# The last channel block of the second mixer matmul, from seven-product sums to ordinary products

## The chip, the cores and the metric

The kernel runs on one core of one Trainium2 chip. The metric is the device time of one execution in microseconds (us); a run's time is that of the core. Five engines work side by side, each through its own queue in order: TensorE (PE, matmuls; PEld is its weight load), VectorE (DVE), ScalarE (ACT), GpSimd (POOL) and SyncE (SP, which here only issues DMAs). TensorE's clock is granted at one of two levels, 1.2 and 2.4 GHz; the profile gives the granted clock as a share of the higher one.

## The reference, cut to what matters

One layer of a decoder trunk is computed for 1024 prompt tokens and 32 sample tokens (8 samples of 4), with a gate per channel that is one number for the prompt and one for each sample. The change lies in the last line:

```python
x = x + gate1 * jnp.dot(mixed, w_o)
xn2 = rms_norm(x, norm2_g) * (1 + scale2) + shift2
hid = jax.nn.relu(jnp.dot(xn2, w_mlp_in))          # 1024 -> 4096 channels
x = x + gate2 * jnp.dot(hid * hid, w_mlp_out)      # 4096 -> 1024 channels
```

## The kernel before

All tensors are held transposed: channels on the 128 partitions, the T = 1056 tokens along the free axis. A float32 product is computed as three faster ones: each operand is split into a rounded high part and the rest (hi, lo), and hi·hi, hi·lo and lo·hi are summed in PSUM. ACT makes the high part (a cast), DVE or POOL subtracts it to get the low part.

Most large matmuls use a seven-product scheme on 2x2 blocks (Strassen's, in Winograd's form): seven products of sums and differences of blocks instead of eight products of the blocks. The sums of the weight blocks are made by POOL (L228 to L231) and split by ACT and DVE (L157, L161, tile wprod); `products_to` keeps this three products ahead of TensorE.

The second mixer matmul takes the 4096 hidden channels in NBLK = 8 blocks of 512. The squared hidden rows lie in DRAM (`hid_d`); `fetch` loads a block of them as quarters (tile hraw: two channel tiles of 128 by two token quarters of H = 264), and `prepare` makes the seven operands of a block out of them: `comb` (POOL, L1562) forms the differences, `high` (ACT, L1550) and `low` (DVE L1558, or POOL L1555 for the products in POOL_LOW) split them. A block is two jobs, x = 0 and 1, for output channels 0 to 511 and 512 to 1023. A job runs its seven products n = 0 to 6; a product is four PSUM groups (two output tiles j, two token halves p) of six matmuls with 264 columns (L1690 to L1692), so 24 matmuls, 168 in a job and 336 in a block. The groups go round eight PSUM banks (`tags`). The result of each group is added to a sum in SBUF, `acc[x, n]`: ACT copies it there in block 0, DVE adds it in later blocks (L1701). So each of the 14 sums runs over all eight blocks.

At the end the sums of a job have to be joined into four outputs each and added to the residual stream: the table FIN gives each step a slot and an engine. Steps j1, j6, j3, k6, j4, k2, j5 add or subtract two sums (`join`, L1624 for a whole page of 1056 columns, L1626 for halves), m1, m6, m2, m5 multiply by the gate (ACT L1605, and DVE L1608 for the 32 sample columns), a1, a6, a2, a5 add the result to the rows y1 of the output (`add`, L1612), s0 and s1 store the rows (L1638). y1[m] holds 128 output channels of the residual stream, loaded from DRAM by `load_y1` (L1588). In the last block, product 6 skips its sum: `gated` (L1593, L1597, L1601) multiplies PSUM by the gate and adds it to y1.

What sets the order: a plan that maps slots to steps. There are two slots to a product, 28 to a block; `tick(s)` writes the steps of slot s into the queues right after the matmuls of that slot, and each engine then runs its queue in order. In block b the operands of block b + 1 are prepared. Pages of 1056 columns come from a pool of NPG = 34; a page is used again once its last reader is done. `copy` issues one of 48 copies of the caches from DRAM to DRAM, 2.1 MB each in this stage, one at each of the last jobs.

`residual` (L1713, L1717, L1721) is what the attention's output projection uses to add a PSUM tile of 352 columns, times a gate, to rows of the stream: one instruction from PSUM, and for the third of the three column tiles two small ones for the samples. `gemm` (L376) runs an ordinary product as hi·hi, hi·lo, lo·hi for each channel tile, with 352 columns, its PSUM tiles here in the three banks of tag g. `prep_to` loads and splits a weight slab for it (L192 on ACT, L196 on DVE, tiles whi and wlo).

Of the kernel before, what the change touches and what calls it, by code (L numbers as in the profile page):

```python
# [17 lines left out]
P = 128  # L18
# [18 lines left out]
NBLK = 8  # L37
NG = 4
# [3 lines left out]
    (("j1", 3, "p"), ("m1", 8, ""), ("a1", 9, "p"), ("j6", 5, "p"), ("j3", 7, "d"), ("k6", 8, "pd"), ("m6", 12, ""), ("a6", 13, "d"),  # L42
     ("j4", 14, "p"), ("k2", 15, "p"), ("j5", 18, "p"), ("m2", 19, ""), ("a2", 21, "dp"), ("m5", 21, ""), ("a5", 22, "d"),
     ("s0", 14, ""), ("s1", 22, "")),
    (("j1", 3, "dp"), ("m1", 6, ""), ("a1", 11, "p"), ("j6", 5, "p"), ("j3", 7, "d"), ("k6", 10, "p"), ("m6", 10, ""), ("a6", 12, "dp"),
     ("j4", 10, "pd"), ("k2", 10, "d"), ("j5", 14, "dp"), ("m2", 11, ""), ("a2", 12, "p"), ("m5", 14, ""), ("a5", 15, "d"),
     ("s0", 14, ""), ("s1", 15, "")),
# [3 lines left out]
class Trunk:  # L51
# [374 lines left out]
    # ---- constants, adaLN modulation, first norm  # L426
# [215 lines left out]
    # ---- input projection  # L642
# [230 lines left out]
    # ---- attention over the prompt  # L873
# [168 lines left out]
    # ---- attention of the samples  # L1042
# [218 lines left out]
    # ---- whole program  # L1261

    def run(self):
# [39 lines left out]
        srcs += [(t["w_mlp_out"][2 * i], t["w_mlp_out"][2 * i + 1]) for i in range(2 * NBLK)]  # L1303
# [6 lines left out]
        # projection: gates and convolution  # L1310
# [17 lines left out]
        # projection: queries, keys, values  # L1328
# [37 lines left out]
        # convolution and attention outputs, gated  # L1366
# [62 lines left out]
        # output projection, residual, second norm  # L1429
# [73 lines left out]
        # channel mixer  # L1503
# [27 lines left out]
        raw, ops, acc, plan = {}, {}, {}, {}  # L1531

# [7 lines left out]
        def fetch(b, q):  # L1540
            if b < NBLK:
# [10 lines left out]
        def low(b, n, q):  # L1552
            h, l = ops[b, n]
            if n in POOL_LOW and (b < NBLK - 1 or n < 5):
# [27 lines left out]
        for b in range(1, NBLK):  # L1582
            prepare(b, 28 * b - 16, 4)
        y1 = {}
# [4 lines left out]

        def gated(m, c, n, src):  # L1590
            y = y1[m][:, c:c + n]
            k = min(n, NP - c)
            nc.vector.scalar_tensor_tensor(out=y[:, :k], in0=src[:, :k], scalar=gate2[:, m, 0:1], in1=y[:, :k],  # L1593
                                           op0=ALU.mult, op1=ALU.add)
            if k < n:
                tmp = self.sm.tile([P, NB, NT], F32, name="rs", tag="rs", bufs=2)
                nc.vector.tensor_tensor(  # L1597
                    out=tmp, in0=src[:, k:n].rearrange("p (b t) -> p b t", t=NT),
                    in1=gate2[:, m, 1:9].unsqueeze(2).to_broadcast([P, NB, NT]), op=ALU.mult)
                ys = y[:, k:n].rearrange("p (b t) -> p b t", t=NT)  # L1600
                nc.vector.tensor_tensor(out=ys, in0=ys, in1=tmp, op=ALU.add)  # L1601
# [33 lines left out]
        def store(x, i):  # L1635
            for j in range(2):
                m = 4 * x + 2 * i + j
                nc.sync.dma_start(out=t["yT"][:, m, :], in_=y1[m])  # L1638

        for x in range(2):  # L1640
# [7 lines left out]
                "a5": lambda x, e: adds(x, e, 5, 1, 0), "s0": lambda x, e: store(x, 0), "s1": lambda x, e: store(x, 1),  # L1648
            }
            for k, s, e in FIN[x]:  # L1650
                at(28 * NBLK - 28 + 14 * x + s, lambda x=x, e=e, f=steps[k]: f(x, e))
# [7 lines left out]
        self.last_prod = 7 * (self.npair + 4 * NBLK - NG // 2)  # L1659
# [46 lines left out]
        for s in sorted(plan):  # L1706
            tick(s)
# [213 lines left out]
```

## Time and profile before

| | |
|---|---|
| time, median of 3 runs | 2211.82 us |
| the 3 runs | 2204.81, 2211.82, 2216.55 us |
| the profiled execution: span from first to last instruction | 2215.5 us (its own time isn't given apart) |
| PE busy | 2064.9 us, 93% |
| DVE busy | 1445.6 us, 65% |
| ACT busy | 1002.2 us, 45% |
| POOL busy | 810.3 us, 37% |
| mean granted TensorE clock | 0.970 |
| second mixer matmul, first to last matmul | 1832.3 to 2200.4 us |
| from there to the end | 15.1 us |

The page shows shares over the whole span; the second mixer matmul is the last 383 us, and there the shares are others: it is read by windows of that stretch. A busy PE is not the same as a PE at full pace, since the ends of matmuls are modelled; its pace is read from the starts of matmuls that follow each other. An instruction of DVE can start while the one before it drains, so a row of equal instructions takes less than the sum of their durations; an instruction that is slowed by another engine shows as a longer instruction, not as idle time.

### The profile page before, as it was taken

To read this page: it belongs to the slowest core of one execution; us is meant where nothing else is said; L and a number is where in the kernel's file an instruction comes from. 1 tells how busy PE (TensorE), PEld (TensorE's weight loads), DVE (VectorE), ACT (ScalarE), POOL (GpSimd) and SP (SyncE) were. 2 spreads that over 40 slices of the span, in tenths; PEclk is the share of its full clock that TensorE was granted. 3 is DMA by queue.
4 is the path that set the end of the run, shared out by engine and by line. 5 is a ranking of instruction groups with operands and counts; after the bars stand their busy time and mean duration, and the time that the engine had idled before them with its cause. 6 is when DMAs were issued, how large, how long until landed. Compare 5 with 4: busy or idle time off the path is not lost.

```text
span 2215.5 us, 39124 instructions
## 1 busy us (share of the span) xinstructions
PE 2064.9 (93%) x15140; PEld 1915.1 (86%) x15140; DVE 1445.6 (65%) x3012; ACT 1002.2 (45%) x2204; POOL 810.3 (37%) x566
## 2 busy tenths in 40 slices
PE   5799999999999989999998799998999999999995
PEld 2799999889888878788787689988999999999995
DVE  4846666345556556666776568378444447999998
ACT  4532323335555645555455223255555557333332
POOL 3636565321111111100112114235333326887876
PEclk8999999999999999999999899999999999999997
DMA  7232221663144667765558985432356546564543
GB/s 278 81 121 77 60 78 60 230 232 112 48 54 54 44 145 135 148 122 106 159 137 138 207 253 175 158 122 106 107 211 240 220 167 229 198 230 172 188 164 118
DMA packets 182291, 325.87 MB, mean 147 GB/s; under 512 B 77144, under 2 KB 122456, under 8 KB 181080
## 3 DMA queue, kind: packets, MB, share of 16 engines
q1 hardware_dynamic: 181672, 323.17, 51.2%
q8 instruction: 119, 1.95, 0.5%
q14 instruction: 68, 0.56, 0.1%
q10 hardware_dynamic: 432, 0.20, 0.0%
HBM read 270.48 MB, written 112.07 MB: 173 GB/s over the span
## 4 chain that ended last, share of the span: by engine, by line
PE 48%; DVE 18%; DMA 9%; ACT 4%; issue 3%; SPq 1%; POOL 1%; another core or an unknown queue 0%; ACTq 0%; DVEq 0%; POOLq 0%
PE ps_g L376 20%; DVE acc L1701 4%; DVE wprod L161 3%; PE ps_g L263 3%; DMA st_d<-st 3%; PE ps_g L265 3%; PE ps_s L264 3%; PE ps_s L263 3%; PE ps_s L265 3%; PE ps_g L264 3%; DVE hl L1558 2%; PE ps_s L975 1%; PE ps_o L1012 1%; DVE wlo L196 1%; DMA rel<-in_rel 1%
## 5 line engine op out<-in xcount | busy, mean ns | idle before, releaser
L161 DVE TENSOR_TENSOR wprod<-wraw,wprod 128x512 fp32r<-128x512 f32 x288 | 281.4, 979 | 177.3 <-ACT wprod L157 177.1
L376 PE MATMUL ps_g<-xh,whi 128*128 128x352 f32 x1056 | 367.9, 348 | 12.4 <-ACT whi L192 4.9
L376 PE MATMUL ps_g<-xh,wlo 128*128 128x352 f32 x1056 | 346.8, 328 | 6.0 <-DVE wlo L196 5.9
L376 PE MATMUL ps_g<-xl,whi 128*128 128x352 f32 x1056 | 347.4, 329 | 2.7 <-POOL xl L405 1.8
L376 PEld LDWEIGHTS ps_g<-xh,whi 128*128 128x128 f32 x1056 | 203.3, 193 | 48.9 <-issue 25.3
L157 ACT CAST wprod<-wraw 128x512 fp32r<-128x512 f32 x288 | 170.3, 618 | 165.4 <-DVE wprod L161 113.2
L376 PEld LDWEIGHTS ps_g<-xh,wlo 128*128 128x128 f32 x1056 | 203.0, 192 | 7.5 <-DVE wlo L196 7.5
L376 PEld LDWEIGHTS ps_g<-xl,whi 128*128 128x128 f32 x1056 | 203.4, 193 | 6.1 <-POOL xl L405 3.7
L161 POOL TENSOR_TENSOR lo<-qn,hi 128x1024 fp32r<-128x1024 f32 x12 | 32.9, 2743 | 364.7 <-ACT hi L157 341.6
L196 DVE TENSOR_TENSOR wlo<-wraw,whi 128x512 fp32r<-128x512 f32 x176 | 127.9, 768 | 45.6 <-PE ps_g L376 25.4
L276 POOL TENSOR_TENSOR ps_z<-ps_z,ps_s 128x264 f32<-128x264 f32 x64 | 60.4, 946 | 251.8 <-DVE ps_s L275 251.8
L263 PE MATMUL ps_s<-th,wprod 128*128 128x264 f32 x512 | 145.7, 285 | 1.8 <-DVE ps_s L275 1.8
L263 PE MATMUL ps_g<-th,wprod 128*128 128x264 f32 x512 | 146.8, 287 | 0.0
L264 PE MATMUL ps_s<-tl,wprod 128*128 128x264 f32 x512 | 145.9, 285 | 0.0
L265 PE MATMUL ps_g<-th,wprod 128*128 128x264 f32 x512 | 145.8, 285 | 0.0
L264 PE MATMUL ps_g<-tl,wprod 128*128 128x264 f32 x512 | 145.5, 284 | 0.0
L265 PE MATMUL ps_s<-th,wprod 128*128 128x264 f32 x512 | 145.4, 284 | 0.0
L983 ACT ACTIVATE S<-S,ng 128x128 f32<-128x128 f32 (+1 forms) x192 | 84.9, 443 | 98.8 <-DVE ng L980 95.9
L192 ACT CAST whi<-wraw 128x512 fp32r<-128x512 f32 x176 | 100.0, 619 | 51.2 <-DMA wraw<-in_w_conv_out 36.7
L263 PE MATMUL ps_g<-xh,wprod 128*128 128x264 f32 x384 | 110.6, 288 | 4.1 <-ACT wprod L157 4.1
L263 PE MATMUL ps_s<-xh,wprod 128*128 128x264 f32 x384 | 110.8, 289 | 3.4 <-DVE ps_s L279 3.4
L265 PE MATMUL ps_g<-xh,wprod 128*128 128x264 f32 x384 | 110.1, 287 | 3.5 <-DVE wprod L161 3.5
(385 smaller groups left out, 6718.1 us busy)
## 6 DMA issues: line engine op xcount, KB each, us to landing
wraw<-in_w_in SPq DMA_DIRECT2D x76, 512.0 KB
wada<-in_w_ada SPq DMA_DIRECT2D x48, 512.0 KB
hid_d<-hid SPq DMA_DIRECT2D x32, 528.0 KB
hraw<-hid_d SPq DMA_DIRECT2D x64, 264.0 KB
wraw<-in_w_mlp_in SPq DMA_DIRECT2D x32, 512.0 KB
wraw<-in_w_mlp_out SPq DMA_DIRECT2D x32, 512.0 KB
kv<-in_v SPq DMA_DIRECT2D x28, 512.0 KB
wraw<-in_w_conv_out SPq DMA_DIRECT2D x24, 512.0 KB
```

The lines of the kernel that those rows point to most:

```text
L157: nc.scalar.copy(hi, src)
L161: eng.tensor_tensor(out=lo, in0=src, in1=hi.bitcast(F32), op=ALU.subtract)
L192: self.nc.scalar.copy(hi[:, s], w[:, s])
L196: self.nc.vector.tensor_tensor(out=lo[:, s], in0=w[:, s], in1=hi[:, s].bitcast(F32), op=ALU.subtract)
L263: nc.tensor.matmul(ps, hi, xh, start=(k == 0), stop=False)
L264: nc.tensor.matmul(ps, hi, xl, start=False, stop=False)
L265: nc.tensor.matmul(ps, lo, xh, start=False, stop=(k == 3))
L276: nc.gpsimd.tensor_tensor(out=z[p], in0=z[p], in1=s[p], op=ALU.add)
L376: self.nc.tensor.matmul(ps, a, x, start=(i == 0), stop=(i == n - 1))
L983: nc.scalar.activation(s, s, AF.Exp, bias=ng[:, hh:hh + 1], accum_out=sm[:, hh:hh + 1])
L1558: nc.vector.tensor_tensor(out=l[:, s], in0=raw[b, q][:, s], in1=h[:, s].bitcast(F32), op=ALU.subtract)
L1701: nc.vector.tensor_tensor(out=a, in0=a, in1=ps, op=ALU.add)
```

## The change

The last of the eight blocks leaves the seven-product scheme. Its products are now ordinary ones, 24 tiles of 12 matmuls with 352 columns (288 in place of 336 with 264), in the order of output rows m = 4, 5, 6, 7, 0, 1, 2, 3, three column tiles each. `residual` adds each tile, times the gate, straight from PSUM to y1[m]. The hidden rows of that block are loaded as they are (`fetch_last`) and split once (`split_last`, two low parts on DVE, two on POOL); there are no differences to form. Its weights are four single slabs, split by `prep_to`, in place of 14 product weights.

The sums of the seven products now run over seven blocks (NSB = 7), and the steps that join them are spread from slot -12 to slot 15 around the start of the ordinary products: those of x = 0 from 12 slots ahead of it, those of x = 1 from tile 7 on. Joins work on whole pages now, each on one engine. `gated` is gone: all sums are whole. Rows are stored after the tile that ends them, the last row in three pieces. The copies of the caches keep their number; since there are two jobs fewer, jobs 0 and 1 issue two each.

The diff, without lines that are only comments, and with two rows of the table:

```diff
+NSB = NBLK - 1
 FIN = (
-    (("j1", 3, "p"), ("m1", 8, ""), ("a1", 9, "p"), ("j6", 5, "p"), ("j3", 7, "d"), ("k6", 8, "pd"), ("m6", 12, ""), ("a6", 13, "d"),
...
+    (("j1", -12, "p"), ("j6", -10, "p"), ("m1", -9, ""), ("a1", -6, "p"), ("j3", -1, "d"), ("k6", 0, "p"), ("j4", 1, "d"), ("k2", 2, "p"),
...
-        srcs += [(t["w_mlp_out"][2 * i], t["w_mlp_out"][2 * i + 1]) for i in range(2 * NBLK)]
+        srcs += [(t["w_mlp_out"][2 * i], t["w_mlp_out"][2 * i + 1]) for i in range(2 * NSB)]
+        srcs += [(t["w_mlp_out"][4 * NSB + i],) for i in (2, 3, 0, 1)]
...
+        END = 28 * NSB
...
-            if n in POOL_LOW and (b < NBLK - 1 or n < 5):
+            if n in POOL_LOW:
...
+        def fetch_last(q):
+            raw[NSB, q] = self.page("hraw")
+            nc.sync.dma_start(out=raw[NSB, q], in_=self.hid_d[4 * NSB + q])
+
+        def split_last(q):
+            v = raw.pop((NSB, q))
+            h, l = last[q] = self.page("hh", dt=F32R), self.page("hl", dt=F32R)
+            if q % 2:
+                self.split(h, l, v, T, lo_on="pool")
+            else:
+                nc.scalar.copy(h, v)
+                for s in (slice(0, 2 * H), slice(2 * H, T)):
+                    nc.vector.tensor_tensor(out=l[:, s], in0=v[:, s], in1=h[:, s].bitcast(F32), op=ALU.subtract)
+
+        for q in range(4):
+            at(END - 26 + 2 * q, lambda q=q: fetch_last(q))
+            at(END - 9 + 2 * q, lambda q=q: split_last(q))
...
-        def gated(m, c, n, src):
...
             for k, s, e in FIN[x]:
-                at(28 * NBLK - 28 + 14 * x + s, lambda x=x, e=e, f=steps[k]: f(x, e))
+                at(END + s, lambda x=x, e=e, f=steps[k]: f(x, e))
...
-            at(28 * (NBLK - 1) + 6 + 2 * m, lambda m=m: load_y1(m))
+            at(END - 11 + 2 * m, lambda m=m: load_y1(m))
+            if m > 3:
+                at(END + 13 + m, lambda m=m: store(m))
...
-        for i in range(2 * NBLK):
+        for i in range(2 * NSB):
...
-            copy(1)
+            copy(2 if i < 2 else 1)
...
+                if n == 5:
+                    self.prep_to(ji + 1)
...
-                        elif b == NBLK - 1 and n == 6:
-                            m, c = 4 * x + j, (2 * p + 1) * H
-                            gated(m, c, H, ps)
...
-        for s in sorted(plan):
-            tick(s)
+        for n, (m, ch) in enumerate([(m, ch) for m in (4, 5, 6, 7, 0, 1, 2, 3) for ch in range(NCH)]):
+            j, s = m % 2, slice(ch * CH, (ch + 1) * CH)
+            ps = self.bank("g")
+            self.gemm(ps[:, :CH], self.wt[ji], [4 * (q // 2) + 2 * j + q % 2 for q in range(4)],
+                      [tuple(v[:, s] for v in last[q]) for q in range(4)])
+            self.residual(y1[m], ps, gate2, m, ch)
+            del ps
+            if j == 0 and ch == 1:
+                self.prep_to(ji + 1)
+            tick(END + n)
+            if m == 3:
+                store(m, s)
+            elif m < 3 and ch == 2:
+                store(m)
+            if j and ch == 2:
+                self.wt.pop(ji)
+                ji += 1
+            self.slot()
```

Where instructions stand. DVE before, in the last block: a low part of a product weight (L161), then the four sums of one product (L1701, their inputs the PSUM banks), and now and then a split of a hidden operand (L1558) or a join (L1624).

```order
L1558 TENSOR_TENSOR hl<-hraw,hh 128x528 x2
L161 TENSOR_TENSOR wprod<-wraw,wprod 128x512
L1701 TENSOR_TENSOR acc<-acc,ps_s 128x264
L1701 TENSOR_TENSOR acc<-acc,ps_pt 128x264
L1701 TENSOR_TENSOR acc<-acc,ps_g 128x264
L1701 TENSOR_TENSOR acc<-acc,ps_o 128x264
L1624 TENSOR_TENSOR acc<-acc 128x1056
```

DVE after, from the last sums to the sixth tile: L1736, L1740 and L1744 are `residual`, L195 the low part of a weight slab, L1631 a join, L1615 the gate of the samples.

```order
L1707 TENSOR_TENSOR acc<-acc,ps_o 128x264
L1631 TENSOR_TENSOR acc<-acc 128x1056
L1736 SCALAR_TENSOR_TENSOR y_24024<-ps_g,modT,y_24024 128x352 x2
L195 TENSOR_TENSOR wlo<-wraw,whi 128x512 x2
L1631 TENSOR_TENSOR acc<-acc 128x1056
L1736 SCALAR_TENSOR_TENSOR y_24024<-ps_g,modT,y_24024 128x320
L1740 TENSOR_TENSOR rs<-ps_g,modT 128x32
L1744 TENSOR_TENSOR y_24024<-y_24024,rs 128x32
L1615 TENSOR_TENSOR acc<-acc,modT 128x32 x2
L1736 SCALAR_TENSOR_TENSOR y_24059<-ps_g,modT,y_24059 128x352
L1631 TENSOR_TENSOR acc<-acc 128x1056
L1736 SCALAR_TENSOR_TENSOR y_24059<-ps_g,modT,y_24059 128x352
```

So between the readers of PSUM there now stand joins of 1056 columns, in place of the lows of product weights of 512.

POOL before, in the last block: differences of hidden quarters and their lows, the sums of weight blocks, then the joins.

```order
L1562 TENSOR_TENSOR hraw<-hraw 128x1056
L1555 TENSOR_TENSOR hl<-hraw,hh 128x1056
L1624 TENSOR_TENSOR acc<-acc 128x1056 x2
L1626 TENSOR_TENSOR acc<-acc 128x528
L1612 TENSOR_TENSOR y_24193<-y_24193,acc 128x2x264
L1612 TENSOR_TENSOR y_24238<-y_24238,acc 128x2x264
L228 TENSOR_TENSOR ws_24300<-wraw 128x512
```

POOL after, from the first joins on; the two L160 are the lows of `split_last`.

```order
L1631 TENSOR_TENSOR acc<-acc 128x1056 x2
L160 TENSOR_TENSOR hl<-hraw,hh 128x1056
L1619 TENSOR_TENSOR y_23846<-y_23846,acc 128x2x264
L1619 TENSOR_TENSOR y_23891<-y_23891,acc 128x2x264
L160 TENSOR_TENSOR hl<-hraw,hh 128x1056
L1631 TENSOR_TENSOR acc<-acc 128x1056 x2
L1619 TENSOR_TENSOR y_23846<-y_23846,acc 128x2x264
L1619 TENSOR_TENSOR y_23891<-y_23891,acc 128x2x264
L1619 TENSOR_TENSOR y_23932<-y_23932,acc 128x2x264
L1619 TENSOR_TENSOR y_23976<-y_23976,acc 128x2x264
L1631 TENSOR_TENSOR acc<-acc 128x1056 x2
```

The last pair of joins (of x = 1) and six more adds behind it run beside tiles 7 to 15; the weight blocks' sums are gone from here.

SP at the start of the second mixer matmul, before, and then the same stretch after (out_sk is a copy of a cache):

```order
L1727 DMA out_sk<-in_k3T 32x16384
L1516 DMA hid_d<-hid 128x1056 x2
L179 DMA wraw<-in_w_mlp_out 128x1024 x2
L1544 DMA hraw<-hid_d 128x2x264 x8
L1727 DMA out_sk<-in_k3T 32x16384
L179 DMA wraw<-in_w_mlp_out 128x1024 x2
```

```order
L1750 DMA out_sk<-in_k3T 32x16384 x2
L1516 DMA hid_d<-hid 128x1056 x2
L178 DMA wraw<-in_w_mlp_out 128x1024 x2
L1545 DMA hraw<-hid_d 128x2x264 x8
L1750 DMA out_sk<-in_k3T 32x16384 x2
L178 DMA wraw<-in_w_mlp_out 128x1024 x2
```

Two copies stand where one stood, ahead of the loads of the next weights and of block 1's hidden quarters.

## Rows read from the trace of the kernel before

**Rows 1.** Windows: us, length, busy us (instructions) per engine, PEclk, DMA share, GB/s
```profile
2052.00:2095.00 43.00, 41.43 (x339) 41.18 (x338) 43.00 (x77) 15.03 (x21) 34.73 (x17) 1.00 0.56 199
2136.10:2200.40 64.30, 49.17 (x338) 46.54 (x336) 63.65 (x94) 17.88 (x27) 50.65 (x27) 0.89 0.31 110
2200.40:2215.50 15.10, 0.00 (x0) 0.00 (x0) 9.44 (x17) 2.67 (x4) 5.18 (x4) 0.50 0.36 144
```

**Rows 2.** Timeline of PE: start us, duration us; first and last matmul, last block
```profile
2136.14 0.28 PE L1690 MATMUL ps_g<-hh,wprod 128*128 128x264 f32 x1
...
2199.94 0.42 PE L1692 MATMUL ps_o<-hh,wprod 128*128 128x264 f32 x1
```

**Rows 3.** What PE waited for, 2136 to 2201 us: total us, times, longest
```profile
PE ps_s L1690 <- DVE acc L1701: 6.2, 4, 3.2
PE ps_g L1691 <- DVE hl L1558: 2.8, 2, 1.7
PE ps_g L1690 <- DVE acc L1701: 2.8, 1, 2.8
```

**Rows 4.** Timeline of PE: a wait in the last block, and matmuls after it
```profile
2155.96 0.56 PE L1690 MATMUL ps_s<-hh,wprod 128*128 128x264 f32 x1 [3.15 <-DVE acc L1701]
2156.32 0.42 PE L1691 MATMUL ps_s<-hl,wprod 128*128 128x264 f32 x1
...
2158.74 0.41 PE L1690 MATMUL ps_g<-hh,wprod 128*128 128x264 f32 x1
```

**Rows 5.** The chain that ended last: one product's four sums on DVE
```profile
2140.28 1.36 DVE acc L1701 x4
```

**Rows 6.** Timeline of PE: matmuls of 352 columns, 24 starts apart
```profile
1353.76 0.32 PE L376 MATMUL ps_g<-oh,wlo 128*128 128x352 f32 x1
...
1357.62 0.32 PE L376 MATMUL ps_g<-oh,wlo 128*128 128x352 f32 x1
```

**Rows 7.** Windows: the attention's output products (L376, 12 matmuls to a tile)
```profile
1340.00:1360.00 20.00, 20.00 (x126) 20.00 (x125) 15.99 (x30) 6.34 (x14) 9.77 (x10) 1.00 0.45 142
```

**Rows 8.** Source lines: instructions, duration ns min/median/max, first and last start us
```profile
L1713 DVE SCALAR_TENSOR_TENSOR x<-ps_g,modT,x x24: 533/578/585, 1387.8 to 1484.0; 128x352 f32<-128x352 f32 x16, 128x320 f32<-128x320 f32 x8
L1721 DVE TENSOR_TENSOR x<-x,rs x8: 191/192/261, 1451.5 to 1484.7; 128x32 f32<-128x32 f32 x8
L1624 POOL TENSOR_TENSOR acc<-acc x7: 2414/2480/2923, 2148.5 to 2191.9; 128x1056 f32<-128x1056 f32 x7
L1624 DVE TENSOR_TENSOR acc<-acc x3: 1245/1258/2166, 2156.9 to 2200.3; 128x1056 f32<-128x1056 f32 x3
L1612 POOL TENSOR_TENSOR y<-y,acc x8: 1292/1593/1769, 2159.9 to 2204.6; 128x528 f32<-128x528 f32 x8
L1612 DVE TENSOR_TENSOR y<-y,acc x8: 692/708/2269, 2175.5 to 2210.1; 128x528 f32<-128x528 f32 x8
L196 DVE TENSOR_TENSOR wlo<-wraw,whi x176: 674/685/2893, 42.0 to 1525.7; 128x512 fp32r<-128x512 f32 x176
```

**Rows 9.** Timeline of the last block: two adds on DVE, and POOL beside them
```profile
2191.90 2.76 POOL L1624 TENSOR_TENSOR acc<-acc 128x1056 f32<-128x1056 f32 x1 [2.10 <-DVE acc L1624]
...
2192.96 4.00 DVE L1612 TENSOR_TENSOR y<-y,acc 128x528 f32<-128x528 f32 x2
...
2194.74 1.65 POOL L1626 TENSOR_TENSOR acc<-acc 128x528 f32<-128x528 f32 x1
```

**Rows 10.** Timeline: the last work of the kernel, on DVE and SP
```profile
2209.48 1.33 DVE L1612 TENSOR_TENSOR y<-y,acc 128x528 f32<-128x528 f32 x2 [0.80 <-ACT acc L1605]
2210.26 1.04 SPq L1638 DMA_DIRECT2D out_yT<-y  x2
```

**Rows 11.** Windows: start of the second mixer matmul, block 0
```profile
1830.00:1840.00 10.00, 6.71 (x49) 6.22 (x48) 7.56 (x9) 4.40 (x11) 7.63 (x5) 0.91 0.11 46
...
1850.00:1860.00 10.00, 10.00 (x85) 10.00 (x84) 7.08 (x6) 7.85 (x21) 8.36 (x6) 1.00 0.98 368
```

**Rows 12.** Timeline of SP in block 0: copies of the caches
```profile
1823.02 0.58 SPq L1727 DMA_DIRECT2D out_sk<-in_k3T  x1
...
1848.86 0.59 SPq L1727 DMA_DIRECT2D out_sk<-in_k3T  x1
```

More of the change, by code (lines that the diff above doesn't have):

```diff
@@ L41 @@
 FIN = (
-    (("j1", 3, "p"), ("m1", 8, ""), ("a1", 9, "p"), ("j6", 5, "p"), ("j3", 7, "d"), ("k6", 8, "pd"), ("m6", 12, ""), ("a6", 13, "d"),
[L43 to L47, printed above, removed]
[4 rows of a table added]
 )
@@ L1540, in fetch @@
         def fetch(b, q):
-            if b < NBLK:
+            if b < NSB:
                 v = raw[b, q] = self.page("hraw")
@@ L1564, in prepare @@
         def prepare(b, s0, d):
-            if b == NBLK:
+            if b == NSB:
                 return
@@ L1581, in run @@
         prepare(0, -8, 2)
-        for b in range(1, NBLK):
+        for b in range(1, NSB):
             prepare(b, 28 * b - 16, 4)
+        last = {}
+        def fetch_last(q):
[13 more added lines that the diff above has]
+            at(END - 9 + 2 * q, lambda q=q: split_last(q))
         y1 = {}
@@ L1588, in load_y1 @@
             nc.sync.dma_start(out=y1[m], in_=self.x1_d[m])
-        def gated(m, c, n, src):
[L1591 to L1601, printed above, removed]
         def scale(m, a, t):
@@ L1633, in adds, with store @@
             both(eng, lambda e, j: add(4 * x + 2 * i + j, part(x, n, j), t, e))
[L1635 to L1638, printed above, removed]
+        def store(m, s=slice(0, T)):
+            nc.sync.dma_start(out=t["yT"][:, m, s], in_=y1[m][:, s])
         for x in range(2):
@@ L1647, in run @@
                 "j5": lambda x, e: join(x, e, 5, 0, 5, ALU.subtract), "m5": lambda x, e: scales(x, 5, 1, 0),
-                "a5": lambda x, e: adds(x, e, 5, 1, 0), "s0": lambda x, e: store(x, 0), "s1": lambda x, e: store(x, 1),
+                "a5": lambda x, e: adds(x, e, 5, 1, 0),
             }
             for k, s, e in FIN[x]:
-                at(28 * NBLK - 28 + 14 * x + s, lambda x=x, e=e, f=steps[k]: f(x, e))
+                at(END + s, lambda x=x, e=e, f=steps[k]: f(x, e))
         def copy(n):
@@ L1658, in run @@
         self.plain_tiles(base, "x2", hidden)
-        self.last_prod = 7 * (self.npair + 4 * NBLK - NG // 2)
+        self.last_prod = 7 * (self.npair + 2 * NBLK - NG // 2 + 2 * NSB)
         ji = base + NG
@@ L1705, in run @@
             ji += 1
-        for s in sorted(plan):
-            tick(s)
+        for n, (m, ch) in enumerate([(m, ch) for m in (4, 5, 6, 7, 0, 1, 2, 3) for ch in range(NCH)]):
[16 more added lines that the diff above has]
+            self.slot()
+        assert not plan
     def residual(self, x, ps, gate, m, c):
```

3 rows, old and new, of the table FIN are left out of this document.

## Prediction

> **What bounds the kernel now.** I read first the windows of the second mixer matmul. In a block of the steady state (the first row of [rows 1]) DVE is busy for all 43.0 us and PE for 41.43, so both are close to their limits, and PE idles 1.6 us. The 339 matmuls recorded there give 41.43/339 = 0.122 us each, so 336 need 41.1 us. The last block is different: in the second row, 64.3 us for the same matmuls, with DVE busy for 63.65. From its first matmul at 2136.14 to the last, which ends at 2200.36 [rows 2], there are 64.2 us, and then 15.1 us without a matmul until the end (the third row of [rows 1]). Together 79.4 us come behind block 6. Next come PE's waits there [rows 3]: every large one is for DVE, the three shown sum to 11.8 us, the smaller ones to 3.2. So 41.1 are products and 15.0 waits; the other 8 us go with the granted clock, 0.89 in that window. How is seen in [rows 4]: PE waited 3.15 us, and behind that the matmuls start 0.22 us apart ((2158.74 - 2156.32)/11) in place of 0.122. That is the 1.2 GHz level; the pace comes back after about 3 us. The reader should see that the end of this kernel is set by DVE, which in the last block sums, joins and prepares all at once, and that PE pays twice for it.
>
> **What goes, and what comes.** The change replaces those 79.4 us. I add up its own version from the start of block 7.
>
> (1) *Start of the ordinary products.* Block 6 no longer prepares seven operands and three product weights ahead; it gets four operands, a weight slab and the first joins instead. On DVE that is two to three instructions fewer of some 0.69 us, on POOL 14 instructions in place of 16. PE can gain at most its idle 1.6 us of a block, at least nothing; I take 0.6, nearer to nothing, since DVE stays almost full. The ordinary products start at 2135.5.
>
> (2) *Their pace on PE.* Matmuls of 352 columns start (1357.62 - 1353.76)/24 = 0.161 us apart [rows 6]. 288 of them take 46.3 us, 1.93 to a tile. That is 5.2 us more than the 41.1 that the seven-product block needs: on PE alone the change is a loss. That tiles of 12 can run without a gap is seen in the attention's output products, which have the same tiles, the same three banks and two DVE instructions to a tile: PE 20.00 of 20.00 us, DVE 15.99 [rows 7].
>
> (3) *DVE beside them.* Only three banks hold the tiles, so tile 18 cannot start before DVE has added tile 15, and behind tile 15 DVE has little left to do besides the tiles. So I count DVE's queue up to that point, with the durations of [rows 8]: 16 tiles x 0.578 = 9.2; 10 small ones for the samples (0.19) 1.9; 8 joins x 1.258 = 10.1; 2 adds x 0.708 = 1.4; 8 small gates at 0.19, an upper value from the same shape, 1.5; 6 weight lows x 0.685 = 4.1. Sum 28.2. Durations overlap: four sums of 0.417 take 1.36 [rows 5], 0.08 less each, so 50 instructions take 24 us. In front of them DVE is behind by some of the 5.5 us that it is behind now (block 6's last sums end on DVE at 2141.64 [rows 5], PE began block 7 at 2136.14 [rows 2]); with POOL quiet in the last slots I take 3.
>
> (4) *What POOL costs DVE.* In [rows 9] two adds on DVE that take 0.708 us each alone [rows 8] took 4.00. The first ends when POOL's join (2191.90 to 2194.66) is over, the second after POOL's next one (2194.74 to 2196.39). So an instruction of DVE with two SBUF operands waits for the POOL instruction under way, and they take turns. Sums that read PSUM keep their 0.417. In the steady block DVE's own work is 56 x 0.34 + 14 x 0.61 + 6 x 0.63 = 31.4 us of 43.0, so it waited 11.6 us beside 34.7 us of POOL [rows 1], a third. In the last block the same counting gives 45 us own of 63.65 + 9.44 busy, 28 of waiting beside 55.8 of POOL, a half. Until tile 15 the changed kernel has on POOL 4 joins x 2.48 and 8 adds x 1.59 [rows 8], 22.6 us. The bounds are nothing and 22.6; at a third it is 7.5, at a half 11.3. I take the half, from the stage with the same joins. DVE reaches tile 15 at 3 + 24 + 11.3 = 38.3 us; PE could start tile 18 at 18 x 1.93 = 34.7. PE loses 3.6 us, and the phase takes 49.9.
>
> The Trainium skill says of this ("SBUF — State Buffer", section "SBUF: two separate sides") that a DVE instruction with two SBUF inputs and a GpSimd instruction take a shared pair of ports as an exclusive lock for the whole instruction, and the other fully blocks. The trace agrees [rows 9]. Read strictly it speaks against putting joins on both engines beside the products, and its result is rival B below.
>
> (5) *New waits.* Page reuse makes the load of row m = 4 wait for POOL's second add of the joins of x = 0, and the first tile's addition waits for that load; all of DVE is queued behind it. The add stands six slots (9 us) ahead and the tile takes 1.93 us, which hides a load of 0.54 MB (1.5 us at the 368 GB/s of [rows 11]) with room; I take 0, at most 3. On SP the loads no longer stand behind stores. ACT has the gates and six weight casts, far below its time.
>
> (6) *The end.* Behind the last matmul: one addition 0.58, two small ones 0.19 each, then the store. Now the end comes 4.7 us after DVE's last instruction (2210.81 to 2215.5 [rows 10]) with two stores of 0.54 MB. The last store is a third of one, 4.3 us is my estimate between 4.0 and 4.7. Sum 5.3, in place of 15.1. The other rows are stored while tiles run: seven rows of 0.54 MB, five of them in the last 12 us, 7.3 us at 368 GB/s.
>
> (7) *The two copies moved to block 0.* 2.1 MB each, 5.7 us at 368 GB/s. One follows the copy issued at 1823.02 [rows 12], into a stretch with 46 GB/s [rows 11]: hidden. The other follows that of 1848.86, into 10 us with a DMA share of 0.98: it delays the weights of the next job. Their first use is some 10 us behind their issue, so I take 0; at most 5.7 for each.
>
> Sum: 2135.5 + 49.9 + 5.3 = 2190.7, 24.8 us below the span of 2215.5. The runs of the kernel lie around a median of 2211.8, 3.7 below that span; what lies around a span isn't shown, so I carry the difference over: **2187 us**.
>
> **The rivals.** A: *DVE keeps up.* The share of a third of the steady block holds, 3 + 24 + 7.5 = 34.5 is under 34.7, PE runs through. 2135.5 + 46.3 + 5.3 = 2187.1, 28.4 less: 2183. For it: [rows 7]. Against: joins of 1056 columns hold DVE and POOL longer than anything there.
>
> B: *The joins lock DVE out.* Every one of POOL's 22.6 us costs DVE the same. Tile 15 is added at 49.6, PE loses 14.9, the phase takes 61.2: 2202.0, 13.5 less: 2198. For it: both adds waited in [rows 9]. Against: DVE is slowed only where it has SBUF work, and POOL's adds wait for gates of ACT at times when DVE reads PSUM.
>
> C: *Slower: PE falls to the lower clock level and stays there.* With three banks only, DVE frees them in bursts; PE waits 3.15 us as in [rows 4], does three tiles at 0.22 x 352/264 = 0.293 us a matmul, 10.6 us, and waits again. Eight such rounds take 110 us: 2250.8, 35 us more: 2247. The kernel would be slower from the fourth round of the eight on ((74.7 - 46.3)/7.9). Against: in [rows 4] the lower level lasted some 3 us, and at 3.5 us a tile DVE catches up. The Trainium skill ("TensorE: Matmul & The Clock Gate", "Part 1: The HAM clock gate") calls the throttled state the default, which activity lifts; by that rule C would need PE to be idle again and again.
>
> D: *The change costs what it moves.* Both copies of (7) delay block 0 in full, 11.4 us: 2198. Against: 46 GB/s in [rows 11].
>
> **How the numbers follow.** Forecast (2184 to 2192) 0.55, A 0.20, B 0.12, D 0.05, C 0.03, other 0.05. About 0.5%, 11 us, is what a measurement here can tell from no change, so 2200.8 is the border. B and D lie just under it; I give each a third above it. Faster 0.88, within 0.5% 0.08, slower 0.04. The range reaches from A less 4 us, since the runs of before already differ by 12, to 2200: 2179 to 2200, with 0.1 above and 0.1 below.
>
> **What would show it.** In the changed profile: the ordinary products start about 43 us behind block 6's first matmul; PE waits in them are for DVE's additions (L1736) and come between tiles 8 and 18; DVE's joins (L1631) are longer than 1.26 us where POOL runs; the granted clock stays near 1.0; from the last matmul to the end some 5 us. I am wrong if the products wait for weights or for a row's load, if block 0 grows by over 2 us, or if clock and waits look like the old last block.

## The result, and the profile after

The changed kernel takes 2188.66 us (median of 4 runs, 2182.63 to 2189.4), the kernel before 2211.96 (4 runs, 2204.81 to 2216.55). The ratio is 0.9887, 95% interval 0.9856 to 0.9917, so the change makes the kernel faster by 1.1%. The forecast was 2187 us, with a range of 2179 to 2200.

The total is a blunt yardstick here. In the profiled executions of this kernel and of all those below, the first matmul of the second mixer matmul starts anywhere from 1811.7 to 1832.3 us, though the program ahead of it is the same. The two executions profiled for the comparison differ by 34.6 us in their spans (2215.45 and 2180.84), and 13.9 of these lie ahead of this matmul (1832.32 and 1818.38). So I compare from here on the *stage*: from the first matmul of the second mixer matmul to the end of the span. It took 383.1 us before and takes 362.5 after, 20.7 less. When the changed kernel ran again later, its stage took 362.4.

Windows of the changed kernel, columns as in [rows 1]: blocks 0 to 5, block 6, the ordinary products, and what follows the last matmul:

```profile
1818.40:2079.20 260.80, 249.01 (x2018) 246.86 (x2017) 247.50 (x407) 112.82 (x193) 204.20 (x95) 1.00 0.62 217
2079.20:2124.40 45.20, 41.87 (x339) 41.27 (x337) 45.20 (x75) 17.46 (x25) 38.53 (x19) 1.00 0.49 157
2124.40:2177.10 52.70, 48.46 (x288) 46.00 (x288) 44.46 (x70) 11.39 (x18) 27.31 (x14) 1.00 0.30 119
2177.10:2180.80 3.70, 0.00 (x0) 0.00 (x0) 0.84 (x3) 0.00 (x0) 0.00 (x0) 1.00 0.16 59
```

The same windows of the kernel before, blocks 0 to 5 and block 6 (the rest stands in [rows 1]):

```profile
1832.30:2093.00 260.70, 251.11 (x2018) 249.39 (x2017) 247.52 (x407) 112.79 (x193) 204.17 (x95) 0.99 0.58 204
...
2093.00:2136.10 43.10, 41.47 (x338) 41.22 (x338) 43.10 (x77) 15.04 (x21) 34.83 (x17) 1.00 0.52 185
```

Read from the starts of the matmuls, the stage splits as follows:

| us | before | after | change | forecast |
|---|---|---|---|---|
| blocks 0 to 5 | 260.7 | 260.9 | +0.1 | 0 |
| block 6 | 43.1 | 45.1 | +2.0 | -0.6 |
| last block | 64.2 | 52.7 | -11.5 | -14.3 |
| last matmul to the end | 15.1 | 3.8 | -11.3 | -9.8 |
| stage | 383.1 | 362.5 | -20.7 | -24.8 |

The clock is 1.00 in all of it, where it was 0.89 in the old last block. PE's waits from the start of the ordinary products on are these, all for DVE (columns as in [rows 3]); the third stands ahead of the first tile:

```profile
PE ps_g L375 <- DVE rs L1740: 2.2, 3, 0.9
PE ps_g L375 <- DVE y L1736: 1.9, 3, 1.4
PE ps_g L375 <- DVE acc L1707: 0.6, 1, 0.6
```

The 24 tiles start 1.92 to 2.0 us apart up to tile 5 and again from tile 17 on. From tile 5 to tile 17 the 12 distances sum to 29.3 us in place of 12 x 1.93 = 23.2, so nearly all the loss, 6.1 us, lies there. DVE's timeline in that stretch, with POOL's instructions beside it behind (start us, duration us; in brackets the idle time before and who ended it):

```profile
2128.49 0.58 DVE L1736 SCALAR_TENSOR_TENSOR y<-ps_g,modT,y 128x352 f32<-128x352 f32 x1 [0.23 <-PE ps_g L375]
2128.99 2.55 DVE L195 TENSOR_TENSOR wlo<-wraw,whi 128x512 fp32r<-128x512 f32 x2
...
2133.30 1.99 DVE L1744 TENSOR_TENSOR y<-y,rs 128x32 f32<-128x32 f32 x1
...
2145.84 1.28 DVE L195 TENSOR_TENSOR wlo<-wraw,whi 128x512 fp32r<-128x512 f32 x2
...
2152.83 2.37 DVE L1631 TENSOR_TENSOR acc<-acc 128x1056 f32<-128x1056 f32 x1 [1.60 <-POOL acc L1631]
...
2163.02 0.17 DVE L1740 TENSOR_TENSOR rs<-ps_g,modT 128x32 f32<-128x32 f32 x1
2163.23 0.89 DVE L1744 TENSOR_TENSOR y<-y,rs 128x32 f32<-128x32 f32 x1
2164.04 0.57 DVE L1736 SCALAR_TENSOR_TENSOR y<-ps_g,modT,y 128x352 f32<-128x352 f32 x1
```

```profile
2127.91 2.48 POOL L1631 TENSOR_TENSOR acc<-acc 128x1056 f32<-128x1056 f32 x1 [8.38 <-DVE acc L1631]
2132.79 2.46 POOL L1631 TENSOR_TENSOR acc<-acc 128x1056 f32<-128x1056 f32 x1 [2.40 <-DVE acc L1631]
...
2150.32 2.48 POOL L1631 TENSOR_TENSOR acc<-acc 128x1056 f32<-128x1056 f32 x1 [5.47 <-DVE acc L1631]
```

Three things are to be seen. Two weight lows take 2.55 us beside POOL's join; at 2145.84, where POOL is idle, such a pair takes 1.28. An addition of 32 columns takes 1.99 us in place of 0.19 [rows 8]: POOL's join from 2132.79 to 2135.25 is under way. And once DVE stands still for 1.60 us, because its join needs the one that POOL has just made. The addition that reads PSUM, at 2128.49, keeps its 0.58 us in the middle of a join on POOL.

The last instructions answer to [rows 10]:

```profile
2176.77 0.32 PE L375 MATMUL ps_g<-hh,wlo 128*128 128x352 f32 x1
2177.12 0.55 DVE L1736 SCALAR_TENSOR_TENSOR y<-ps_g,modT,y 128x320 f32<-128x320 f32 x1 [1.33 <-PE ps_g L375]
...
2177.81 0.19 DVE L1744 TENSOR_TENSOR y<-y,rs 128x32 f32<-128x32 f32 x1
2178.03 0.33 SPq L1643 DMA_DIRECT2D out_yT<-y  x1
```

Nothing but the last tile's addition and a third of a row's store is left behind the last matmul.

### The profile page after: what moved, and what is told of

The parts are those of the page before. It is cut to its first block, busy times and chain, and to the rows that moved or that the text cites. A ratio compares the mean times of both kernels' runs of the same rounds, so it can differ in the third digit from the quotient of the medians.

```text
span 2180.8 us, 38933 instructions
## 1 busy us (share of the span) xinstructions
PE 2055.5 (94%) x15092; PEld 1906.9 (87%) x15092; DVE 1416.5 (65%) x2973; ACT 995.9 (46%) x2195; POOL 785.4 (36%) x553
## 3 DMA queue, kind: packets, MB, share of 16 engines
q8 instruction: 118, 1.93, 0.5%
## 4 chain that ended last, share of the span: by engine, by line
PE 52%; DVE 18%; DMA 5%; ACT 4%; issue 3%; SPq 1%; POOL 1%; another core or an unknown queue 0%; DVEq 0%; ACTq 0%; POOLq 0%
PE ps_g L375 23%; DVE acc L1707 5%; DVE wprod L160 4%; PE ps_g L262 3%; PE ps_s L262 3%; PE ps_s L263 3%; PE ps_g L264 3%; PE ps_s L264 3%; PE ps_g L263 3%; PE ps_o L1011 1%; DVE hl L1559 1%; PE ps_s L974 1%; DVE wlo L195 1%; DMA st_d<-st 1%; DMA sg<-gate_d 1%
## 5 line engine op out<-in xcount | busy, mean ns | idle before, releaser
L160 DVE TENSOR_TENSOR wprod<-wraw,wprod 128x512 fp32r<-128x512 f32 x276 | 269.9, 980 | 177.1 <-ACT wprod L156 176.9
L156 ACT CAST wprod<-wraw 128x512 fp32r<-128x512 f32 x276 | 163.3, 618 | 151.8 <-DVE wprod L160 104.6
L195 DVE TENSOR_TENSOR wlo<-wraw,whi 128x512 fp32r<-128x512 f32 x184 | 132.1, 760 | 47.6 <-PE ps_g L375 22.3
L160 POOL TENSOR_TENSOR lo<-qn,hi 128x1024 fp32r<-128x1024 f32 x12 | 34.0, 2833 | 358.0 <-ACT hi L156 332.9
L191 ACT CAST whi<-wraw 128x512 fp32r<-128x512 f32 x184 | 104.5, 619 | 54.8 <-DMA wraw<-in_w_conv_out 40.3
```

The lines of the kernel that those rows point to most:

```text
L156: nc.scalar.copy(hi, src)
L160: eng.tensor_tensor(out=lo, in0=src, in1=hi.bitcast(F32), op=ALU.subtract)
L191: self.nc.scalar.copy(hi[:, s], w[:, s])
L195: self.nc.vector.tensor_tensor(out=lo[:, s], in0=w[:, s], in1=hi[:, s].bitcast(F32), op=ALU.subtract)
```

## The experiments

Four kernels ran on one chip, four on a second, three on a third. Ratios are to the kernel before on the same chip; lengths of the stage and its parts come from the one trace that each run left. "Phase" is the time from the first ordinary product to the end of the last.

### Both kernels without their joins

```diff
-FIN = (
...
+FIN = ((), ())
```

In the kernel before only the stores are kept:

```diff
 FIN = (
-    (("j1", 3, "p"), ("m1", 8, ""), ("a1", 9, "p"), ("j6", 5, "p"), ("j3", 7, "d"), ("k6", 8, "pd"), ("m6", 12, ""), ("a6", 13, "d"),
...
+    (("s0", 14, ""), ("s1", 22, "")),
...
+    (("s0", 14, ""), ("s1", 15, "")),
```

> The changed kernel with the table of join steps empty: the sums of the seven products are not joined, gated or added, so that part of the output is left out. All else stays. I read the stage from the second mixer matmul's first matmul to the end (383.1 us before, 362.5 after), which leaves the earlier stages out. Theory (the joins beside the tiles are what is left of the old tail's cost): block 6 falls from 45.1 back to about 43.0 us, the ordinary products from 52.7 to about 46.5, the end stays near 3.8; stage 354. Rival (DVE is held by the tiles' own additions, or PE by three banks alone): the products stay above 50, stage 360.

> The kernel before with the join steps left out in the same way (product 6 is still added to the output, the stores stay). Theory (the joins made the old last block long and the end late): the last block falls from 64.2 to 43 to 46 us, the end from 15.1 to about 5, stage 383.1 -> about 352 to 355, level with the changed kernel without joins or a little below, since its products take 41 us of PE and not 46. Rival (the preparation of seven operands and 14 product weights is what was saved): the last block stays above 55 us, and the stage above 365.

Windows of the changed kernel without joins: block 6, phase, end; then of the kernel before without joins: last block, end.

```profile
2079.90:2123.90 44.00, 41.66 (x338) 41.23 (x337) 44.00 (x76) 16.08 (x23) 28.80 (x15) 1.00 0.48 162
2123.90:2170.20 46.30, 46.26 (x290) 45.97 (x288) 20.91 (x50) 2.28 (x4) 0.00 (x0) 1.00 0.34 134
2170.20:2173.90 3.70, 0.00 (x0) 0.00 (x0) 0.84 (x3) 0.00 (x0) 0.00 (x0) 0.88 0.15 55
```

```profile
2115.60:2160.70 45.10, 42.27 (x338) 41.33 (x336) 41.35 (x86) 10.09 (x15) 17.66 (x11) 1.00 0.44 158
2160.70:2167.60 6.90, 0.02 (x1) 0.00 (x0) 0.55 (x2) 0.00 (x0) 0.00 (x0) 0.84 0.77 309
```

Both kernels leave part of the output out, and each ran once. The stages take 354.7 and 355.9 us; the second lies 0.9 us above what I expected, since its end takes 6.9 us and not about 5. Without joins the change is worth 1.2 us, with them 20.7. The phase takes 46.24 us, PE without a gap, where [rows 6] gave 46.3; the seven-product block takes 45.15 us. So the joins cost 383.1 - 355.9 = 27.2 us before, and 362.5 - 354.7 = 7.7 after, and this difference of 19.5 us is nearly all of the gain. By themselves the ordinary products bring next to nothing. With the joins they bring two things: all sums are whole one block earlier, so that the joins have work of PE to lie beside, and DVE has room for them there. Without joins it is busy for 20.91 of the phase's 46.3 us, where it is busy for 41.35 of 45.1 in the old last block. Which of the two counts for more no run here separates. Block 6 is 43.97 us here: 1.15 of its loss belongs to the early steps that stand in it (two joins, their gate and addition), the remaining 0.9 does not.

### The joins on one engine

All joins and additions from the start of the phase on go to DVE; POOL keeps those of block 6. The rows of x = 0 for all:

```diff
...
-    (("j1", -12, "p"), ("j6", -10, "p"), ("m1", -9, ""), ("a1", -6, "p"), ("j3", -1, "d"), ("k6", 0, "p"), ("j4", 1, "d"), ("k2", 2, "p"),
-     ("m6", 2, ""), ("j5", 3, "d"), ("a6", 3, "p"), ("m2", 4, ""), ("a2", 5, "p"), ("m5", 5, ""), ("a5", 6, "d")),
...
+    (("j1", -12, "p"), ("j6", -10, "p"), ("m1", -9, ""), ("a1", -6, "p"), ("j3", -1, "d"), ("k6", 0, "d"), ("j4", 1, "d"), ("k2", 2, "d"), ("m6", 2, ""), ("j5", 3, "d"), ("a6", 3, "d"), ("m2", 4, ""), ("a2", 5, "d"), ("m5", 5, ""), ("a5", 6, "d")),
...
```

> The changed kernel with every join and add from slot 0 on given to DVE; POOL has nothing to do beside the tiles. Theory (each instruction of POOL blocks DVE's two-SBUF-operand ones): DVE takes on 4 joins x 1.17 and 8 adds x 0.63 = 9.7 us more work before tile 15 and loses some 11 us of waiting; tile 15 is added at about 37 to 39 us of the phase in place of 40.2, the phase takes 49 to 52.7 us, the kernel is 0 to 4 us faster than the changed one (2185 to 2189). DVE's joins take 1.25 us each, without exception. Rival (DVE's longer instructions have another cause, such as the DMA traffic): the phase grows by the 9.7 us to about 62, 2198.

Window of the phase:

```profile
2119.90:2169.30 49.40, 47.34 (x288) 46.16 (x288) 42.84 (x84) 11.40 (x18) 0.00 (x0) 1.00 0.32 127
```

Tile 15's addition starts 35.6 us into the phase and ends at 36.2, a little earlier than expected, where it starts at 39.7 in the changed kernel; the phase takes 49.4, the stage 359.1, the ratio is 0.9889 (0.9854 to 0.9924). DVE does 14 instructions more and is busy for 1.6 us less. The joins take 1.25 us each; the additions come in pairs of 1.32, which is 0.62 apart. From these lengths I estimate: 4 joins x 1.2 + 10 additions x 0.62 = 11 us came to DVE; without them it would have been busy 42.8 - 11 = 31.8, and in the changed kernel 44.46 - 31.8 = 12.7 us were waiting beside POOL's 27.31: a share of 0.46. Taking POOL's help away makes the phase 3.3 us shorter.

### Eight banks, alone and with the joins on DVE

```diff
-            ps = self.bank("g")
+            ps = self.bank(tags[n % 8])
```

> The changed kernel with the tiles of the ordinary products going round all eight PSUM banks, as the seven-product groups do, in place of three. Theory (PE stalls because tile 18 needs the bank of tile 15, which DVE reaches at 40.2 us): PE runs up to eight tiles ahead, its waits in the phase fall from 6.3 us to under 1, the phase takes 46.5 to 48.5 us, 4 to 6 us faster than the changed kernel (2183 to 2185). Rival (PE's waits come from the weight slabs or operands): no change, 2188.

> The changed kernel with both single edits at once: the ordinary tiles go over eight banks, and every join and addition of the last 24 tiles is DVE's. Theory (what holds the ordinary products up is DVE's queue: it reaches a tile late, and three banks turn that lateness into a wait at once): with DVE some 35 us of work up to tile 15 instead of 38 and eight tiles of slack, PE waits under 1 us in all; the phase from the first ordinary product to the last takes 46.3 to 47.5 instead of 52.7, the stage from the first product of the second mixer matmul to the end 356 to 357 instead of 362.5. Rival (the weights of the next slab, split on DVE behind joins, become the new wait, as with eight banks alone): phase 48.5 or more, stage above 358.

With eight banks alone the phase takes 50.4 us, the stage 360.1, the ratio is 0.9903 (0.9876 to 0.993). PE runs 18 tiles without a gap, then comes one wait. Windows around it, and the first matmuls behind it:

```profile
2122.20:2158.00 35.80, 35.28 (x218) 35.01 (x218) 33.84 (x49) 10.03 (x16) 23.59 (x12) 1.00 0.15 59
2158.00:2162.00 4.00, 2.25 (x8) 2.25 (x9) 3.97 (x9) 1.36 (x2) 2.51 (x3) 0.68 0.00 0
2162.00:2172.70 10.70, 10.67 (x64) 10.38 (x63) 6.63 (x14) 0.00 (x0) 1.20 (x1) 0.96 0.84 334
```

```profile
2159.75 0.66 PE L375 MATMUL ps_ss<-hh,wlo 128*128 128x352 f32 x1 [2.24 <-DVE wlo L195]
...
2160.21 0.49 PE L375 MATMUL ps_ss<-hh,whi 128*128 128x352 f32 x1
2160.50 0.49 PE L375 MATMUL ps_ss<-hl,whi 128*128 128x352 f32 x1
```

The expectation of waits below 1 us was wrong: DVE is as late as before (tile 15 at 39.7), and what it is late with is now the low parts of the fourth weight slab, which stand in the same queue. The wait of 2.24 us costs more than itself in this trace: behind it the matmuls start 0.29 us apart in place of 0.161, at the 1.2 GHz level, and tile 19 starts 5.8 us after tile 18.

With both edits the loss is gone. Windows of block 6, phase and end:

```profile
2077.30:2122.50 45.20, 41.82 (x339) 41.22 (x337) 45.20 (x75) 17.47 (x25) 38.56 (x19) 1.00 0.48 158
2122.50:2169.00 46.50, 46.50 (x288) 46.23 (x288) 42.63 (x84) 11.41 (x18) 0.00 (x0) 1.00 0.30 118
2169.00:2173.00 4.00, 0.02 (x1) 0.00 (x0) 0.84 (x3) 0.00 (x0) 0.00 (x0) 1.00 0.62 239
```

PE is busy for the whole 46.5 us; the phase is what PE alone needs. The stage takes 356.5, as the theory had it, and the ratio is 0.9878 (0.9856 to 0.9901). Neither edit alone does it: DVE's queue must be short enough for the weights, and the banks must cover its bursts.

### Block 6

Three kernels ask where its 2 us went. The first cuts the two low parts that DVE makes of the last hidden rows over two slots each (`split_last(q, 0)` does the cast and the first half, `split_last(q, 1)` the second); the second has this together with eight banks and the joins on DVE.

```diff
         for q in range(4):
-            at(END - 9 + 2 * q, lambda q=q: split_last(q))
+            if q % 2:
+                at(END - 9 + 2 * q, lambda q=q: split_last(q))
+            else:
+                at(END - 10 + 2 * q, lambda q=q: split_last(q, 0))
+                at(END - 9 + 2 * q, lambda q=q: split_last(q, 1))
```

> The changed kernel, but in block 6 the two low parts that DVE makes of the last hidden rows are each cut over two slots: one half one slot earlier, the other where it stood. The number of instructions is the same. Theory (the 2 us that block 6 lost come from bursts: two lows in a row, 3.4 us beside POOL, and again lows and weight lows in a row at the block's end, while PE has five banks ahead of DVE's sums): block 6 takes 43.0 to 43.6 us instead of 45.1, the phase stays 52 to 53, stage 360.3 to 361. Rival (DVE is simply overfull in block 6, and the order within it does not matter): block 6 stays at 45 and the stage at 362.5.

> All three edits together: eight banks, the last joins and additions on DVE alone, the lows of block 6 in two slots each. Theory (the three losses are separate): block 6 43.3, phase 46.5, 3.8 behind it: stage 354.5, about the time of the changed kernel without any join (354.7), and 0.985 of the time of the kernel before. Rival (what block 6 gains is handed on as a longer queue of DVE at the start of the ordinary products, or the slab's weights are late): stage 356.5 or more.

Both fell: block 6 takes 45.2 us in either, the stages 362.4 and 356.5, the ratios are 0.9891 (0.9866 to 0.9915) and 0.989 (0.985 to 0.9931). The two halves took 2.31 and 1.16 us in their two slots, together about what the pair took in one (3.39). So this burst was not the cause. Then I took these four instructions off DVE, on top of eight banks and the joins on DVE:

```diff
-            if q % 2:
-                self.split(h, l, v, T, lo_on="pool")
-            else:
-                nc.scalar.copy(h, v)
-                for s in (slice(0, 2 * H), slice(2 * H, T)):
-                    nc.vector.tensor_tensor(out=l[:, s], in0=v[:, s], in1=h[:, s].bitcast(F32), op=ALU.subtract)
+            self.split(h, l, v, T, lo_on="pool")
...
-            at(END - 9 + 2 * q, lambda q=q: split_last(q))
+            at(END - 11 + 2 * q, lambda q=q: split_last(q))
```

> The same two edits, and the low parts of the last four hidden rows all on POOL, each two slots earlier; DVE loses four instructions of 0.62 us in block 6, POOL gets two of 2.5 us. Theory (block 6 is limited by DVE's own work plus its waiting beside POOL, not by the order of its instructions: 2.5 us less own work, 1.7 to 2.5 us more waiting beside POOL): block 6 44.2 to 45.2 us, that is hardly better. Rival (the 2 us of block 6 hang on those four instructions that DVE has just in front of the gap): block 6 43.0 to 43.6. If POOL comes late with the last low, PE waits for it at the first ordinary tile.

Windows of block 6, phase and end, then the waits of PE and DVE that are new, and what SP waited for:

```profile
2074.40:2117.40 43.00, 41.40 (x339) 41.16 (x338) 43.00 (x73) 16.18 (x23) 41.29 (x20) 1.00 0.36 116
2117.40:2165.20 47.80, 46.72 (x290) 46.11 (x288) 43.13 (x84) 12.55 (x20) 2.67 (x2) 1.00 0.37 143
2165.20:2171.10 5.90, 0.00 (x0) 0.00 (x0) 0.83 (x3) 0.00 (x0) 0.00 (x0) 0.70 0.75 289
```

```profile
PE ps_g L373 <- POOL hl L158: 1.0, 1, 1.0
```

```profile
DVE y L1729 <- DMA y<-x_d: 2.7, 1, 2.7
```

```profile
SPq L1601 <- POOL hl L158: 23.0, 4, 11.0
```

The rival of this run was right and my theory wrong: block 6 is back at 42.97 us, although POOL is busy there for 41.3 us, more than ever. DVE's four lows, with what they wait beside POOL, were those 2 us. (Two things are changed at once here, the engine and two slots; which of them did it is open.) But the stage takes 357.5 us, 1.1 more than without this edit: POOL comes late with the last low part, which ends at 2120.15. PE waits for it in tile 0, and SP issues the load of a row of y1 (L1601) only at 2120.17; for that load DVE waits 2.7 us. The end grows from 4.0 to 6.0; what lengthens it no run separates. The ratio is 0.9888 (0.986 to 0.9916).

### The kernel before with its joins on DVE

```diff
 FIN = (
-    (("j1", 3, "p"), ("m1", 8, ""), ("a1", 9, "p"), ("j6", 5, "p"), ("j3", 7, "d"), ("k6", 8, "pd"), ("m6", 12, ""), ("a6", 13, "d"),
+    (("j1", 3, "d"), ("m1", 8, ""), ("a1", 9, "d"), ("j6", 5, "d"), ("j3", 7, "d"), ("k6", 8, "d"), ("m6", 12, ""), ("a6", 13, "d"),
...
```

The other rows are changed alike, so that no step is left on POOL.

> The kernel before, with every join and addition that stood on POOL put on DVE; the last channel block stays a seven-product block. Theory (the old end was long because the joins needed the last block's sums and so stood at the very end, whichever engine does them): DVE's own 45 us of the last block grow by some 15 and its waiting beside POOL falls from 28 to 8; last block and end together 74 to 77 us instead of 79.4, stage 377 to 381, ratio to before 0.997 to 0.999. Rival (it was the lock between POOL and DVE that made the old end long, and the change gained by having less POOL work there): last block and end under 66 us, stage under 370.

Last block and end:

```profile
2125.20:2181.10 55.90, 46.21 (x337) 44.01 (x336) 55.73 (x100) 16.44 (x25) 18.33 (x11) 0.94 0.33 121
2181.10:2199.00 17.90, 0.00 (x0) 0.00 (x0) 12.39 (x26) 3.97 (x6) 0.00 (x0) 0.58 0.35 139
```

Last block and end take 73.9 us in place of 79.3 (expected: 74 to 77), the stage 377.7, the ratio is 0.9968 (0.995 to 0.9985). Taking POOL's part of the joins away is worth 5.4 us to the kernel before, a quarter of what the change gains. DVE is still busy for 12.4 us behind the last matmul: as long as the joins need the last block's sums, they stand at the end, whichever engine does them.

### The changed kernel and the best version side by side

> The changed kernel itself once more, as the yardstick for the other two on one chip. Stage from the first product of the second mixer matmul to the end 362.5 us as before, block 6 45.1, phase of the ordinary products 52.7; ratio to the kernel before 0.987 to 0.991.

> Eight banks, and every join and addition of the last 24 tiles on DVE, once more beside the changed kernel on one chip. Theory (the 6 us that the stage became shorter arrive in the total): stage 356.5, median 5 to 7 us under that of the changed kernel. Rival (what comes before this stage changes with the kernel and takes them back): the medians are within 3 us of each other.

On one chip: kernel before 2202.85 us, changed kernel 2180.76 (ratio 0.9907, 0.9884 to 0.9931), eight banks with the joins on DVE 2173.37 (0.9875, 0.9848 to 0.9902). The stages take 362.4 and 356.45, the same as in their first traces to 0.1 us. The medians differ by 7.4 us, a little more than the theory's 5 to 7. The intervals of the totals still overlap; in the traces the 6 us are there both times.

## Why the prediction was right, and where its steps were not

The sum was -24.8 us for the stage; the trace shows -20.7. The two errors that made the forecast too good are 5.5 us, the one that made it too bad is 1.5. The medians came 23.3 us apart, so the forecast of the total came closer than its sum deserved, by luck: a total that moves by 10 us from run to run doesn't tell 21 from 25.

**(1) The start, -0.6 forecast, +2.0 measured: wrong, in sign too.** I had bounded PE's gain at nothing from below; it lost. I compared numbers of instructions. DVE starts 74 in block 6 in place of 76, as forecast; POOL starts 18 in place of 16, where I had counted 14. The step that failed is "on DVE two to three instructions fewer": what counted was what stood on POOL at that time. The runs show what the loss hangs on: 1.15 us on the early joins and additions (gone without joins), and all of it on the four lows that DVE makes of the hidden rows (gone when POOL makes them, two slots earlier). In the changed kernel, with POOL beside it behind, and then in the changed kernel without joins:

```profile
2112.11 3.39 DVE L1599 TENSOR_TENSOR hl<-hraw,hh 128x528 fp32r<-128x528 f32 x2
2115.41 1.80 DVE L160 TENSOR_TENSOR wprod<-wraw,wprod 128x512 fp32r<-128x512 f32 x1
...
2121.36 1.32 DVE L1599 TENSOR_TENSOR hl<-hraw,hh 128x528 fp32r<-128x528 f32 x2
```

```profile
2110.36 2.81 POOL L160 TENSOR_TENSOR hl<-hraw,hh 128x1056 fp32r<-128x1056 f32 x1
2113.13 3.54 POOL L1619 TENSOR_TENSOR y<-y,acc 128x528 f32<-128x528 f32 x2
```

```profile
2113.31 3.59 DVE L1594 TENSOR_TENSOR hl<-hraw,hh 128x528 fp32r<-128x528 f32 x2
2116.83 0.68 DVE L155 TENSOR_TENSOR wprod<-wraw,wprod 128x512 fp32r<-128x512 f32 x1
```

The first pair of lows takes 3.39 us where the second, without POOL beside it, takes 1.32. It takes 3.59 without joins too, beside a low that POOL makes of a hidden row (2113.66 to 2116.34), so the joins are not what holds it. What the early joins and additions lengthen are the lows of the product weights behind it: 1.80 us, and 0.68 without them.

**(2) PE's pace: right.** 46.3 us forecast, 46.24 measured without joins, 46.53 in the best version.

**(3) and (4) DVE beside the products and POOL's price: right in size.** The sums ended 2.2 us into the phase (forecast 3). Up to the end of tile 15's addition DVE was busy for 38.2 us, forecast 38.3 with the half of POOL's time as waiting; over the whole phase that share came out as 0.46 by the estimate above, so neither the third of rival A nor the whole of rival B. In part two misses cancel: POOL is busy for 26.6 us up to there, where I had counted 22.6. The Trainium skill ("SBUF — State Buffer", "SBUF: two separate sides") says that the one that comes second is fully blocked. The trace agrees where DVE has two SBUF operands (1.99 us for 32 columns). That the share stays under one fits with DVE's spending part of POOL's time on tiles from PSUM, as the 0.58 us at 2128.49 show; how much of it that makes isn't shown. What I left out is a wait of DVE for POOL: 1.60 us in which DVE's join needs POOL's (2.0 us idle in all). With it tile 15's addition ends at 40.2 us instead of 38.3.

**The phase, 49.9 forecast, 52.7 measured: one tile too late.** I let tile 18 wait for tile 15. But DVE was late already at tile 14, which has the two small instructions for the samples behind it, and tile 17 needs its bank. That bank comes free at 2163.19 (the end of L1740 above), and tile 17 starts at 2163.34, 39.0 us into the phase in place of 17 x 1.93 = 32.8: this is the loss of 6.2.

```profile
2163.34 0.40 PE L375 MATMUL ps_g<-hh,whi 128*128 128x352 f32 x1 [0.50 <-DVE rs L1740]
```

With my own numbers tile 14 would have been done about 0.6 us ahead of tile 15's end, at 37.7, and the loss would have been 4.9 and not 3.6. So 1.3 of the missing 2.8 us are the wrong tile, another 1.3 are tile 17's start at 39.0 instead of 37.7, and 0.2 are PE's own pace.

**(5) No wait for a row of y1: right.** The first tile's addition starts at 2127.68, right behind a join. But what held the load was not POOL's second add, which is done at 2116.67: SP issues it at 2120.53, behind a weight load that waits until 2120.11 for DVE. The cover was not thick: where the load waits for a later low of POOL, it costs 2.7 us (the last run on block 6).

**(6) The end, 5.3 forecast, 3.8 measured.** The three instructions took the 0.9 us expected. From DVE's last to the end there are 2.8 us and not 4.3, which I had scaled from two stores of a whole row. That the smaller store alone makes this isn't shown: with the lows on POOL the same third of a row takes 5.1 us from there, with a DMA share of 0.75 in the end in place of 0.16.

**(7) The copies: right.** Block 0 takes 47.78 us, before 47.76. Rival D is out. Rival C too: the clock stays at 1.00 in the phase.

**What bounds the kernel: right, but half said.** I argued that DVE sums, joins and prepares all at once in the last block. The runs without joins show which of these was too much: without joins the old last block takes 45.15 us, and DVE is busy for nearly all of it, so it was the joins on top of a queue that was already almost full.

## What to carry to other kernels

Before an ending is made cheaper, take its finishing work out of both versions once: here that showed that the new form of the products was worth 1 us without joins, and that some 20 hang on where the joins stand and on DVE's room beside them. Where an engine runs behind another through few buffers, follow its queue at each buffer up to the last one that is late, and look at what else stands in the same queue (weights, loads), because more buffers alone only move the wait there. And compare the stage in question by the trace when the total scatters by more than the edit is worth.

## What the runs showed of the hardware

- A second engine can be worse than none. POOL did 27.3 us of joins and additions in the phase; DVE does the same in about 11, and the phase is 3.3 us shorter without POOL.
- The stage repeats to 0.1 us between executions (362.46 and 362.40; 356.46 and 356.45), while the time ahead of it, with the same program, varies by 20 us (1811.7 to 1832.3).
- The same wait of PE does not always cost the clock. In block 0 PE waits 3.3 us at the same place in all 13 traces. Behind it the matmuls start 0.22 us apart, at the 1.2 GHz level, in eight of them; 0.12 us apart in three, the changed kernel's first trace among them; and in two they go from 0.12 to 0.22 within some 1 us. Block 0 takes 47.75 to 47.78 us in all 13. The wait in the changed kernel's two traces, the first with 0.12 and the second with 0.22 behind it:

```profile
1825.18 0.36 PE L1699 MATMUL ps_s<-hh,wprod 128*128 128x264 f32 x1 [3.31 <-ACT ps_z L1527]
```

```profile
1822.52 0.56 PE L1699 MATMUL ps_s<-hh,wprod 128*128 128x264 f32 x1 [3.28 <-ACT ps_z L1527]
```

- So the matmuls at the 1.2 GHz level behind a wait of 2.24 us (eight banks alone) and one of 3.15 ([rows 4]) are what one execution of each shows. In the changed kernel's phase the longest wait is 1.4 us, and the granted clock stays at 1.00.
